# First attention of a two-layer diffusion block: two heads in step, row maxima from the high parts on 64 contraction rows

## The chip, the cores and the metric

The kernel runs on one NeuronCore of a Trainium2 chip. The metric is device time in microseconds (us) of one execution, the median of several runs. All products are made in float32 precision by splitting operands into a high part, which the fp32r format of the matmuls holds exactly, and a low part (the rest), and adding up to three products of parts.

## The reference

Two layers over 1024 latent tokens and 256 context tokens, 1024 features each. Each layer modulates its input, mixes the tokens, projects, adds and normalizes, then runs a gated feed-forward with 2816 hidden features, adds and normalizes again. The mixer of layer 0 holds the attention that the change touches: 12 query heads of 64 features share 4 heads of keys and values (three query heads for each).

```python
def gqa_attend(q, k, v):
    s = jnp.einsum('bkgqd,bksd->bkgqs', q, k, preferred_element_type=F32) * (HEAD_DIM ** -0.5)
    p = jax.nn.softmax(s, axis=-1)
    return jnp.einsum('bkgqs,bksd->bkgqd', p.astype(v.dtype), v)
```

Latent queries attend to all 1280 keys, context queries to the 256 context keys. Queries and keys have been normalized and rotated before. A softmax does not depend on what is subtracted from a row of scores; the row maximum is subtracted to keep the exponentials in range.

## The kernel before

One program runs the stages in order: `in0` (input projections of layer 0; it leaves the heads' queries, keys and values in DRAM, as `qs`, `ks` and `v0`, each with its high part in rows 0 to 63 and its low part in rows 64 to 127), `attn0` (the first attention), `out_proj`, `ffn`, and the same for layer 1 with another attention. A scheduler writes the order of the instructions of each engine: it takes them in the order in which the code emits them, as a priority, and puts an instruction whose inputs or buffers are not ready, by its own estimate of times, behind others that are. On the chip each engine then follows that fixed order.

`attn0` works in units of one head and 256 queries, 60 units: 48 of latents with ten tiles of 128 keys, taken as five steps of two tiles, and 12 of context with one step. Within a pair of heads the units alternate between the two heads. Each step has three parts, emitted at different times:

- `most` computes scores query-major, of the high part of q with both parts of k (128 rows of contraction: `q1` holds the high part of q twice, `kst` both parts of k). Step 0 makes two matmuls of 256 context keys (L926), steps 1 to 4 one matmul of 512 keys each (L931). VectorE reduces each bank to negated row maxima (L927, L932). The last step combines them, splits them in two parts, transposes these on TensorE (L945), and ScalarE writes them as rows 64 and 65 of `q2` (L946).
- `expo` computes the scores again, key-major: for each of two key tiles one matmul on 128 rows (L955) and one on 66 (L956, the low part of q and the two rows that take the maxima off). ScalarE makes the exponentials `e` (L958). They are split into high and low parts in `pp`: the high part is copied by GpSimd or ScalarE, the low part subtracted by GpSimd or VectorE, as the step's letters in `HENG0` and `LENG0` say (helpers at L205, L209 and L213).
- `pv` multiplies the parts with the values, three matmuls for each key tile (L972, L973, L974; `va` has the high part of v and 64 columns of ones, which give the sums of a row, `vb` the low part). After the last step `fin` copies the result to SBUF (L984), transposes the row sums with two matmuls that have one row of contraction, at partition 64 (L987), takes their reciprocals, spreads them over 64 partitions with two transposes (L991), multiplies (L995) and, for every second head, splits the two heads' 128 features into `X` on GpSimd.

`most` is emitted 6 steps ahead of `expo` (`LEAD0`) and `pv` 4 steps behind it (`LAG0`). PSUM has 8 banks: 3 for the scores of `most`, 2 for those of `expo`, 1 for the values, 2 for transposes. `load` fetches the queries of a unit, and keys and values when a new head of them begins, on SP's queue. Other work may be emitted between the steps by `pump`, from a queue that `ada_vec` fills; for this stage `ADA0[1]` is empty, and `in0` ends with emptying the queue.

Of the kernel before, what the change touches and what calls it, by code (L numbers as in the profile page):

```python
# [9 lines left out]
F32 = mybir.dt.float32  # L10
# [7 lines left out]
P = 128  # L18
# [34 lines left out]
HENG0, LENG0, LEAD0, LAG0, PB0 = 'gagaa', 'ggvgv', 6, 4, (3, 2, 2)  # L53
# [20 lines left out]
# ------------------------------------------------------------------ host side: layout only  # L74
# [101 lines left out]
class K:  # L176
# [48 lines left out]
    # ---- weights: one unit of [128, 1024] float32 -> exact (h, l) pair  # L225
# [79 lines left out]
    def ada_vec(self, l, v, nvec, srcs, pspool, pstag, bufs=2, q0=0, abufs=None):  # L305
        """queue modulation vector v of layer l (for nvec of the two conditionings), feature-major"""
# [32 lines left out]
    # ---------------------------------------------------------------- residual, layer norm  # L339
# [6 lines left out]
    def acc_load(self, l, c, b):  # L346
        """ALPHA * x of feature chunk c, block b"""
# [12 lines left out]
    def ln_block(self, b, pools, sc=None, sh=None, acc='keep', out=None, lnb=None, eng=None, tiles=None, group=1):  # L360
        """LN of the columns of block b of ACC (normalised token-major, in place): X = split(LN * sc + sh), ACC = ALPHA * LN."""
# [48 lines left out]
    def ln_vecs(self, l, lng, lnb, nvec, ml, vsh, vsc, tag):  # L410
        """per conditioning: s = g * (1 + sc), b' = b * (1 + sc) + sh ; and ALPHA * g, ALPHA * b"""
# [22 lines left out]
    def qk_post(self, wp, pst, ps, tt, dst, h0, norm, tabs, lat, gain):  # L434
        """ps [128, 512] = 2 token tiles x 4 heads x 64; tt the first token tile; writes dst[h0..h0+3]"""
# [50 lines left out]
    def v_post(self, wp, ps, tt, dst, h0, dv, tag="t1", bufs=2):  # L486
        """ps [128, 2 x 256] to dst [head][128 tok][kt]: (h | l) of 64 columns each, or 128 float32 columns"""
# [17 lines left out]
    def tm_mm(self, o, w, kh, i):  # L505
        """256 output columns of token tile i over one half of the contraction; o: a half of a bank"""
# [39 lines left out]
    def early(self, l, pp, wp):  # L546
        """first hidden chunks of the first blocks, beside the last layer norm of the out-projection"""
# [12 lines left out]
    def ffn(self, l, blks):  # L560
# [3 lines left out]
        with tc.tile_pool(name=f"ffn{l}", bufs=1, reuse_waits="tile") as fp:  # L564
# [11 lines left out]
            def hidden(hc):  # L576
                """hidden chunk hc: {block: (h, l) parts}"""
# [26 lines left out]
            # hidden chunks in pairs; the last ones run block by block beside the layer norm  # L604
# [84 lines left out]
    # ---------------------------------------------------------------- out-projection of both mixers  # L689
# [41 lines left out]
    # ---------------------------------------------------------------- layer 0  # L731
    def in0(self):
# [8 lines left out]
        with ExitStack() as es:  # L741
# [35 lines left out]
            # rope tables with the gains: (q, k) x (cos, sin)  # L777
# [16 lines left out]
            # u: pool mixer branch, feature-major  # L794
# [13 lines left out]
            def pool_mat():  # L808
                """grouped pool matrix, in place"""
# [26 lines left out]
    def pool_mix_sums(self, wp, dp, j, u, pin, ped):  # L836
        nc = self.nc
        L = PADL
        if True:
# [13 lines left out]
            # rows that stopped a step earlier lie in the other buffer  # L853
# [11 lines left out]
    def dup_load(self, dst, src):  # L865
        """dst [128, n] = src [64, n] twice"""
# [3 lines left out]
    def pt_mm(self, psg, es_, i):  # L870
        """transposes of key tiles i, i+1 of two query tiles into one bank"""
# [7 lines left out]
    def attn0(self):  # L879
        """Scores twice: query-major (high part of q) for the row maxima, then key-major with the maxima  # L880
        taken off by two more rows of the contraction, so that the exponentials come out key-major."""
        nc, tc = self.nc, self.tc
        with ExitStack() as es:
# [10 lines left out]

            def load(st):
                hd, pr = st['hd'], st['pr']
                kv = hd // 3
                st['q2'] = self.tile(sp, [66, 256], F32R, "q2", bufs=4)
                if kv not in kv_tiles:
                    kst = self.tile(self.kvp, [P, NTOK], F32R, "kst", bufs=2)  # L900
                    self.dma(kst, self.ks[kv])
                    k2 = self.tile(wp, [66, NTOK], F32R, "k2", bufs=2)
                    self.dma(k2[0:64], self.ks[kv, 0:64])
                    self.copy(ONEE[0], k2[64:66], one[64:66, 0:1].to_broadcast([2, NTOK]))
                    va = self.tile(wp, [P, 10, P], F32R, "va", bufs=2)
                    self.dma(va[:, :, 0:64], self.v0[kv, :, :, 0:64])
                    self.copy(ONEE[1], va[:, :, 64:], one.unsqueeze(1).to_broadcast([P, 10, 64]))
                    vb = self.tile(wp, [P, 10, 64], F32R, "vb", bufs=2)
                    self.dma(vb, self.v0[kv, :, :, 64:])
                    kv_tiles[kv] = (kst, k2, va, vb)  # L910
                st['kv'] = kv_tiles[kv]
                st['q1'] = self.tile(self.kvp, [P, 256], F32R, "q1", bufs=4)
                self.dup_load(st['q1'], self.qs[hd, 0:64, pr * 256:pr * 256 + 256])
                self.dma(st['q2'][0:64], self.qs[hd, 64:128, pr * 256:pr * 256 + 256])

            def most(st, i):
                """query-major scores of one bank, its row maxima"""
                if i == 0:
                    load(st)
                    st['m'] = self.tile(sp, [P, 2, 3], F32, "m", bufs=4)  # L920
                S = self.tile(psm, [P, 512], F32, "sm")
                kst = st['kv'][0]
                lhs = lambda t: st['q1'][:, t * P:t * P + P]
                if i == 0:
                    for t in range(2):
                        nc.tensor.matmul(S[:, t * 256:t * 256 + 256], lhsT=lhs(t), rhs=kst[:, NLAT:], start=True, stop=True)  # L926
                    nc.vector.tensor_reduce(out=st['m'][:, :, 0], in_=S.rearrange("p (t k) -> p t k", t=2), axis=AX.X, op=ALU.max,  # L927
                                            negate=True)
                else:
                    t, k = (i - 1) // 2, (i - 1) % 2  # L930
                    nc.tensor.matmul(S, lhsT=lhs(t), rhs=kst[:, k * 512:k * 512 + 512], start=True, stop=True)  # L931
                    nc.vector.tensor_reduce(out=st['m'][:, t, 1 + k:2 + k], in_=S, axis=AX.X, op=ALU.max, negate=True)  # L932
                if i == st['np'] - 1:
                    with tc.high_priority(HP0) if HP0 else ExitStack():
                        if i:
                            m = self.tile(sp, [P, 2], F32, "mm", bufs=4)
                            nc.vector.tensor_reduce(out=m, in_=st['m'], axis=AX.X, op=ALU.min)
                        else:
                            m = st['m'][:, :, 0]
                        r = self.tile(sp, [P, 2, 2], F32R, "mr", bufs=4)  # L940
                        nc.vector.tensor_copy(out=r[:, :, 0], in_=m)
                        nc.vector.tensor_tensor(out=r[:, :, 1], in0=m, in1=r[:, :, 0].bitcast(F32), op=ALU.subtract)
                        S = self.tile(psr, [P, 512], F32, "r")
                        for t in range(2):
                            nc.tensor.transpose(S.bitcast(F32R)[0:2, t * P:t * P + P], r[:, t, :], self.identr)  # L945
                        nc.scalar.copy(out=st['q2'][64:66], in_=S[0:2, :256])  # L946

            def expo(st, i):
                """key-major scores less the maxima, exponentials, their parts"""
                kst, k2 = st['kv'][:2]  # L950
                S = self.tile(pss, [P, 512], F32, "ss")
                for a in range(2):
                    k = (st['k0'] + 2 * i + a) * P
# [374 lines left out]
```

## Time and profile before

| | |
|---|---|
| time, median of 3 runs | 3291.66 us (3290.71 to 3294.64) |
| span of the profiled execution | 3289.0 us |
| its own time beside the span | not recorded; the median is 2.7 us above the span |
| TensorE busy (matmuls) | 3193.6 us, 97% |
| TensorE weight loads | 2815.5 us, 86%, beside the matmuls |
| VectorE, ScalarE, GpSimd busy | 55%, 31%, 41% |
| granted TensorE clock, mean | 0.984 of full speed |
| first attention | about 288 to 705 us |

The profile lists instructions by line, engine, operation and tile. Busy time is the time covered by an engine's recorded instructions. A matmul's record runs to the modelled end of its results, and the next one starts earlier than that, so the distance between starts says more of TensorE's pace than the recorded length. A matmul of fp32 data appears as two records, a weight load (PEld) and the matmul (PE).

### The profile page before, as it was taken

The numbers are of one execution on the slowest core, as the hardware profiler recorded it, in microseconds if no ns is written. First come the engines' busy times: TensorE is split into PE (matmuls) and PEld (weight loads), VectorE is DVE, ScalarE is ACT, GpSimd is POOL, SyncE is SP. The second block draws the span as 40 slices with busy tenths as digits, with TensorE's granted clock in tenths as the row PEclk, the third lists the DMA queues.
The fourth block names the chain that finished last, engine by engine and source line by source line (L and its number), as shares of the span: only waits on it lengthen the run. The fifth ranks groups of instructions, "written<-read, shape, count | busy, mean of one in ns | idle before, by whom it ended". The sixth has DMA issues, their size and how long they took to land. (4 is left out here: it accounts for less than half of the span.)

```text
span 3289.0 us, 47600 instructions
## 1 busy us (share of the span) xinstructions
PE 3193.6 (97%) x18820; PEld 2815.5 (86%) x18820; DVE 1825.3 (55%) x3251; ACT 1011.1 (31%) x1800; POOL 1352.9 (41%) x1266
## 2 busy tenths in 40 slices
PE   8899999999999999999999989999999999999997
PEld 8798999988888888888888889988887888888887
DVE  6998777766655444443226696378854323222326
ACT  2235676642310111111113333377842211111111
POOL 3665777761322222222222244267742332232234
PEclk8899999999999999999999999999999999999999
DMA  5354021031222222221112144222320111111111
GB/s 224 108 189 121 28 51 54 28 134 56 89 72 77 78 73 70 70 77 52 39 39 65 66 132 139 92 76 84 90 93 24 58 52 45 52 46 51 45 58 52
DMA packets 142895, 250.60 MB, mean 76 GB/s; under 512 B 25552, under 2 KB 95952, under 8 KB 142544
## 3 DMA queue, kind: packets, MB, share of 16 engines
q1 hardware_dynamic: 142672, 247.55, 23.6%
q8 instruction: 149, 2.44, 0.3%
q14 instruction: 74, 0.61, 0.1%
HBM read 207.91 MB, written 39.58 MB: 75 GB/s over the span
## 5 line engine op out<-in xcount | busy, mean ns | idle before, releaser
L213 POOL TENSOR_TENSOR w<-raw,w 128x1024 fp32r<-128x1024 f32 x120 | 288.1, 2408 | 820.5 <-ACT w L205 572.5
L235 PE MATMUL f<-X,w 128*128 128x512 f32 (+1 forms) x1648 | 607.9, 369 | 1.2 <-ACT ACC L217 1.2
L236 PE MATMUL f<-X,w 128*128 128x512 f32 (+1 forms) x1648 | 605.2, 367 | 0.0
L237 PE MATMUL f<-X,w 128*128 128x512 f32 (+1 forms) x1648 | 604.9, 367 | 0.0
L205 ACT CAST w<-raw 128x1024 fp32r<-128x1024 f32 x176 | 182.4, 1049 | 1019.2 <-issue 615.0
L540 DVE TENSOR_TENSOR sg<-f,sg 128x512 f32<-128x512 f32 (+1 forms) x103 | 65.2, 633 | 589.8 <-ACT sg L539 589.8
L358 DVE SCALAR_TENSOR_TENSOR ACC<-f,mod,ACC 128x512 f32<-128x512 f32 (+1 forms) x400 | 274.1, 695 | 164.3 <-PE f L237 164.2
L235 PEld LDWEIGHTS f<-X,w 128*128 128x128 f32 x1648 | 311.5, 189 | 52.1 <-ACT ACC L217 1.6
L237 PEld LDWEIGHTS f<-X,w 128*128 128x128 f32 x1648 | 311.3, 189 | 51.6
L236 PEld LDWEIGHTS f<-X,w 128*128 128x128 f32 x1648 | 311.5, 189 | 50.3
L513 PE MATMUL acc<-w,X 128*128 128x256 f32 x1008 | 292.9, 291 | 8.5 <-ACT u L802 4.9
L324 DVE SCALAR_TENSOR_TENSOR ada<-adraw,silu_c,ada 128x256 f32<-128x256 f32 x490 | 290.7, 630 | 5.9 <-DMA adraw<-in_ad 2.9
L514 PE MATMUL acc<-w,X 128*128 128x256 f32 x1008 | 291.6, 289 | 0.0
L515 PE MATMUL acc<-w,X 128*128 128x256 f32 x1008 | 291.5, 290 | 0.0
L236 PE MATMUL f<-hid,w 128*128 128x512 f32 (+1 forms) x776 | 283.6, 367 | 0.0
L237 PE MATMUL f<-hid,w 128*128 128x512 f32 (+1 forms) x776 | 283.4, 367 | 0.0
L235 PE MATMUL f<-hid,w 128*128 128x512 f32 (+1 forms) x776 | 282.1, 367 | 0.0
L213 POOL TENSOR_TENSOR hid<-sg,hid 128x512 fp32r<-128x512 f32 (+1 forms) x109 | 132.2, 1213 | 303.4 <-DVE hid L207 292.1
L213 POOL TENSOR_TENSOR pp<-e,pp 128x512 fp32r<-128x512 f32 x156 | 203.8, 1314 | 34.8 <-ACT pp L205 29.0
L513 PEld LDWEIGHTS acc<-w,X 128*128 128x128 f32 x1008 | 198.0, 197 | 9.4 <-ACT u L802 5.1
L514 PEld LDWEIGHTS acc<-w,X 128*128 128x128 f32 x1008 | 198.1, 196 | 0.0
L515 PEld LDWEIGHTS acc<-w,X 128*128 128x128 f32 x1008 | 197.8, 196 | 0.0
(279 smaller groups left out, 7026.4 us busy)
## 6 DMA issues: line engine op xcount, KB each, us to landing
raw<-in_fi SPq DMA_DIRECT2D x88, 512.0 KB, 3.6
adraw<-in_ad SPq DMA_DIRECT2D x86, 512.0 KB, 3.7
raw<-in_fo SPq DMA_DIRECT2D x44, 512.0 KB, 3.6
qs<-stg SPq DMA_DIRECT2D x27, 512.0 KB, 3.9
qd<-qs SPq DMA_DIRECT2D x192, 64.0 KB, 2.3
q<-qs SPq DMA_DIRECT2D x180, 64.0 KB, 2.2
ks<-stg SPq DMA_DIRECT2D x20, 512.0 KB, 3.0
kst<-ks SPq DMA_DIRECT2D x16, 640.0 KB, 4.3
```

The lines of the kernel that those rows point to most:

```text
L205: nc.scalar.copy(out=out, in_=in_)
L213: eng.tensor_tensor(out=out, in0=a, in1=b, op=op)
L235: mm(ps, lhsT=wh, rhs=xh, start=start, stop=False)
L236: mm(ps, lhsT=wh, rhs=xl, start=False, stop=False)
L237: mm(ps, lhsT=wl, rhs=xh, start=False, stop=stop)
L324: nc.vector.scalar_tensor_tensor(out=a, in0=rv[:, k], scalar=s, in1=a, op0=ALU.mult, op1=ALU.add)
L358: self.nc.vector.scalar_tensor_tensor(out=a, in0=ps[:, :n], scalar=g[:, f:f + 1], in1=a, op0=ALU.mult, op1=ALU.add)
L513: mm(o, lhsT=xh, rhs=w[:, 0, k], start=st, stop=False)
L514: mm(o, lhsT=xh, rhs=w[:, 1, k], start=False, stop=False)
L515: mm(o, lhsT=xl, rhs=w[:, 0, k], start=False, stop=sp)
L540: nc.vector.tensor_tensor(out=sg[:, :n], in0=pa[:, :n], in1=sg[:, :n], op=ALU.mult)
```

## The change

The units become pairs of heads: 30 units (24 of latents, 6 of context), each with five or one step, and every step does its work for both heads. `most` uses the high part of k alone, on 64 rows of contraction: the even head's matmul has its operands in partitions 0 to 63, the odd head's in partitions 64 to 127, where `q1` has the second copy of q's high part and a new tile `ku` a copy of k's. The matmuls of the two heads are emitted next to each other, into two banks. Their maxima lie in one tile, so that combining, splitting and transposing come once for both heads. `expo` and `pv` loop over the heads; both heads of a step use the same engines for their parts. The values of the two heads share one bank, half each. `fin` comes once for both heads: one copy of 512 columns, four transposes of sums in one bank and four spreading transposes in another. `LAG0` goes from 4 steps to 2 (steps are twice as large), the `e` tiles from 5 to 3, `q1` and `q2` from 4 of one head to 3 of each head, `os` and `on` from 2 to 1. The call of `pump` in the loop is removed. The rest of the diff takes comments and docstrings out.

```diff
-HENG0, LENG0, LEAD0, LAG0, PB0 = 'gagaa', 'ggvgv', 6, 4, (3, 2, 2)
+HENG0, LENG0, LEAD0, LAG0, PB0 = 'gagaa', 'ggvgv', 6, 2, (3, 2, 2)
...
+            def load_kv(kv):
...
+                ku = self.tile(wp, [P, NTOK], F32R, "ku", bufs=2)
+                self.dma(ku[64:128], self.ks[kv, 0:64])
...
             def most(st, i):
...
-                S = self.tile(psm, [P, 512], F32, "sm")
-                kst = st['kv'][0]
-                lhs = lambda t: st['q1'][:, t * P:t * P + P]
+                S = [self.tile(psm, [P, 512], F32, "sm") for j in range(2)]
+                rows = [slice(0, 64), slice(64, 128)]
+                kh = [st['kv'][0][0], st['kv'][1][2]]
+                lhs = lambda j, t: st['q1'][j][rows[j], t * P:t * P + P]
                 if i == 0:
                     for t in range(2):
-                        nc.tensor.matmul(S[:, t * 256:t * 256 + 256], lhsT=lhs(t), rhs=kst[:, NLAT:], start=True, stop=True)
...
+                        for j in range(2):
+                            nc.tensor.matmul(S[j][:, t * 256:t * 256 + 256], lhsT=lhs(j, t), rhs=kh[j][rows[j], NLAT:],
+                                             start=True, stop=True)
...
                     t, k = (i - 1) // 2, (i - 1) % 2
-                    nc.tensor.matmul(S, lhsT=lhs(t), rhs=kst[:, k * 512:k * 512 + 512], start=True, stop=True)
-                    nc.vector.tensor_reduce(out=st['m'][:, t, 1 + k:2 + k], in_=S, axis=AX.X, op=ALU.max, negate=True)
+                    for j in range(2):
+                        nc.tensor.matmul(S[j], lhsT=lhs(j, t), rhs=kh[j][rows[j], k * 512:k * 512 + 512], start=True, stop=True)
+                    for j in range(2):
+                        nc.vector.tensor_reduce(out=st['m'][:, j, t, 1 + k:2 + k], in_=S[j], axis=AX.X, op=ALU.max, negate=True)
...
             def expo(st, i):
...
+                for j in range(2):
...
-                e = self.tile(wp, [P, 512], F32, "e", bufs=5)
+                    e = self.tile(wp, [P, 512], F32, "e", bufs=3)
...
             def pv(st, i):
...
+                po = [st['po'][:, j * 256:j * 256 + 256] for j in range(2)]
...
+                    for j in range(2):
+                        va, vb = st['kv'][j][3:]
+                        h, l = [st['p'][i, j][:, s, a * 256:a * 256 + 256] for s in range(2)]
+                        nc.tensor.matmul(po[j], lhsT=va[:, k], rhs=h, start=i + a + j == 0, stop=False)
+                        nc.tensor.matmul(po[j][0:64], lhsT=vb[:, k], rhs=h, start=False, stop=False)
+                        nc.tensor.matmul(po[j], lhsT=va[:, k], rhs=l, start=False, stop=i == st['np'] - 1 and a + j == 2)
...
             def fin(st):
...
-                os = self.tile(wp, [P, 256], F32, "os", bufs=2)
-                nc.scalar.copy(out=os, in_=po[:, :256])
+                os = self.tile(wp, [P, 512], F32, "os", bufs=1)
+                nc.scalar.copy(out=os, in_=po)
                 R = self.tile(psr, [P, 512], F32, "r")
-                for t in range(2):
-                    nc.tensor.transpose(R[:, 256 + t:257 + t], os[64:65, t * P:t * P + P], self.ident[64:65, 64:65])
...
+                for t in range(4):
+                    nc.tensor.transpose(R[:, t:t + 1], os[64:65, t * P:t * P + P], self.ident[64:65, 64:65])
...
-            units = [dict(hd=2 * hp + j, pr=pr, k0=0 if pr < 4 else NLAT // P, np=5 if pr < 4 else 1, p={})
-                     for hp in range(6) for pr in range(5) for j in range(2)]
+            units = [dict(hp=hp, pr=pr, k0=0 if pr < 4 else NLAT // P, np=5 if pr < 4 else 1, p={})
+                     for hp in range(6) for pr in range(5)]
...
-                if n % ADA0[2] == 7:
-                    self.pump(1)
```

## Rows read from the trace of the kernel before

**Rows 1.** The page, part 1: busy us (share of the span) xinstructions.
```profile
PE 3193.6 (97%) x18820; PEld 2815.5 (86%) x18820; DVE 1825.3 (55%) x3251; ACT 1011.1 (31%) x1800; POOL 1352.9 (41%) x1266
```

**Rows 2.** Busy time by windows: stretch, length, engines, granted clock, DMA share.
```profile
core 0: us, PE busy (x) PEld busy (x) DVE busy (x) ACT busy (x) POOL busy (x), PEclk, DMA share, GB/s
...
300.00:700.00 400.00, 400.00 (x3128) 374.92 (x3127) 296.91 (x605) 272.85 (x512) 303.85 (x320) 1.00 0.14 37
```

**Rows 3.** Waits, 300 to 705 us: who, for whom; total us, times, longest.
```profile
ACT e L958 <- PE ss L956: 78.2, 127, 2.8
...
DVE m L927 <- PE sm L926: 37.1, 34, 1.9
...
PEld o L974 <- DVE pp L213: 0.2, 1, 0.2
```

**Rows 4.** Timeline of TensorE's matmuls: start us, length us, instruction.
```profile
422.46 0.63 PE L931 MATMUL sm<-kst,q 128*128 128x512 f32 x2
422.94 0.28 PE L955 MATMUL ss<-q,kst 128*128 128x256 f32 x1
423.05 0.29 PE L956 MATMUL ss<-q,k 66*128 66x256 f32 x1
423.17 0.29 PE L955 MATMUL ss<-q,kst 128*128 128x256 f32 x1
423.30 0.28 PE L956 MATMUL ss<-q,k 66*128 66x256 f32 x1
423.51 0.28 PE L987 MATMUL r<-c_ident,os 1*128 1x1 f32 x2
423.72 0.39 PE L972 MATMUL o<-pp,va 128*128 128x256 f32 x1
423.94 0.28 PE L973 MATMUL o<-pp,vb 128*64 128x256 f32 x1
424.06 0.28 PE L974 MATMUL o<-pp,va 128*128 128x256 f32 x1
```

**Rows 5.** Groups by line, 285 to 710 us: busy us, mean ns | idle before.
```profile
L213 POOL TENSOR_TENSOR pp<-e,pp 128x512 fp32r<-128x512 f32 x156 | 203.8, 1314 | 34.8 <-ACT pp L205 29.0 <-DVE m L932 1.3
...
L931 PE MATMUL sm<-kst,q 128*128 128x512 f32 x192 | 73.0, 418 | 2.2 <-DVE m L927 1.5 <-DVE m L932 0.5 <-ACT ps_d L816 0.3
L209 POOL TENSOR_SCALAR pp<-e 128x512 fp32r<-128x512 f32 x108 | 72.7, 674 | 69.8 <-ACT e L958 69.3 <-PE ss L956 0.4
...
L926 PE MATMUL sm<-kst,q 128*128 128x256 f32 x120 | 26.4, 301 | 0.0
```

**Rows 6.** Timeline of TensorE's weight loads in the stretch of rows 4.
```profile
423.18 0.19 PEld L956 LDWEIGHTS ss<-q,k 66*128 66x128 f32 x1
423.51 0.19 PEld L987 LDWEIGHTS r<-c_ident,os 1*128 1x128 f32 x2
423.72 0.19 PEld L972 LDWEIGHTS o<-pp,va 128*128 128x128 f32 x1
```

**Rows 7.** One line, L987: matmuls with first and last start; idle before.
```profile
L987 PE MATMUL r<-c_ident,os x120: 194/217/221, 308.7 to 704.4; 1*128 1x1 f32 x120
...
  issue: 8.0, 32
```

**Rows 8.** Timeline of matmuls where L945 stands between L987's.
```profile
308.37 0.40 PE L931 MATMUL sm<-kst,q 128*128 128x512 f32 x1
308.70 0.22 PE L987 MATMUL r<-c_ident,os 1*128 1x1 f32 x1
308.84 0.28 PE L945 MATMUL r<-identr,mr 128*2 128x128 f32 x2
...
309.43 0.28 PE L973 MATMUL o<-pp,vb 128*64 128x256 f32 x1
```

**Rows 9.** Timeline of VectorE at the attention's start.
```profile
288.09 0.62 DVE L927 TENSOR_REDUCE m<-sm 128x2 f32<-128x512 f32 x1
...
292.82 0.14 DVE L937 TENSOR_REDUCE mm<-m 128x2 f32<-128x6 f32 x1
```

**Rows 10.** DMA issues, 280 to 710 us: count, KB each, us to landing.
```profile
k<-ks SPq DMA_DIRECT2D x4, 320.0 KB, 5.3
```

More of the change, by code (lines that the diff above doesn't have):

```diff
@@ L893, in attn0 @@
             kv_tiles = {}
-            def load(st):
[L896 to L914, printed above, removed]
@@ new lines, in load_kv @@
+            def load_kv(kv):
+                kst = self.tile(self.kvp, [P, NTOK], F32R, "kst", bufs=2)
+                self.dma(kst, self.ks[kv])
+                k2 = self.tile(wp, [66, NTOK], F32R, "k2", bufs=2)
+                self.dma(k2[0:64], self.ks[kv, 0:64])
+                self.copy(ONEE[0], k2[64:66], one[64:66, 0:1].to_broadcast([2, NTOK]))
+                ku = self.tile(wp, [P, NTOK], F32R, "ku", bufs=2)
+                self.dma(ku[64:128], self.ks[kv, 0:64])
+                va = self.tile(wp, [P, 10, P], F32R, "va", bufs=2)
+                self.dma(va[:, :, 0:64], self.v0[kv, :, :, 0:64])
+                self.copy(ONEE[1], va[:, :, 64:], one.unsqueeze(1).to_broadcast([P, 10, 64]))
+                vb = self.tile(wp, [P, 10, 64], F32R, "vb", bufs=2)
+                self.dma(vb, self.v0[kv, :, :, 64:])
+                return kst, k2, ku, va, vb
@@ new lines, in load @@
+            def load(st):
+                pr = st['pr']
+                st['kv'], st['q1'], st['q2'] = [], [], []
+                for j in range(2):
+                    hd = 2 * st['hp'] + j
+                    kv = hd // 3
+                    if kv not in kv_tiles:
+                        kv_tiles[kv] = load_kv(kv)
+                    st['kv'].append(kv_tiles[kv])
+                    q2 = self.tile(sp, [66, 256], F32R, f"q2{j}", bufs=3)
+                    q1 = self.tile(self.kvp, [P, 256], F32R, f"q1{j}", bufs=3)
+                    self.dup_load(q1, self.qs[hd, 0:64, pr * 256:pr * 256 + 256])
+                    self.dma(q2[0:64], self.qs[hd, 64:128, pr * 256:pr * 256 + 256])
+                    st['q1'].append(q1)
+                    st['q2'].append(q2)
@@ L935, in most @@
                         if i:
[L936 removed]
+                            m = self.tile(sp, [P, 2, 2], F32, "mm", bufs=4)
                             nc.vector.tensor_reduce(out=m, in_=st['m'], axis=AX.X, op=ALU.min)
                         else:
[L939 to L941 removed]
@@ L946, in most @@
-                        nc.scalar.copy(out=st['q2'][64:66], in_=S[0:2, :256])
-            def expo(st, i):
[L950 to L953, printed above, removed]
-                    o = S[:, a * 256:a * 256 + 256]
-                    nc.tensor.matmul(o, lhsT=kst[:, k:k + P], rhs=st['q1'], start=True, stop=False)
-                    nc.tensor.matmul(o, lhsT=k2[:, k:k + P], rhs=st['q2'], start=False, stop=True)
-                e = self.tile(wp, [P, 512], F32, "e", bufs=5)
-                nc.scalar.activation(e, S, AF.Exp)
-                p = st['p'][i] = self.tile(wp, [P, 2, 512], F32R, "pp", bufs=6)
-                self.copy(HENG0[i], p[:, 0], e)
-                self.tt(LENG0[i], p[:, 1], e, p[:, 0].bitcast(F32), ALU.subtract)
+                        for j in range(2):
+                            for t in range(2):
+                                o = j * 256 + t * P
+                                nc.tensor.transpose(S.bitcast(F32R)[0:2, o:o + P], r[:, j, t, :], self.identr)
@@ new lines, in most @@
+                        for j in range(2):
+                            nc.scalar.copy(out=st['q2'][j][64:66], in_=S[0:2, j * 256:j * 256 + 256])
+            def expo(st, i):
+                for j in range(2):
+                    kst, k2 = st['kv'][j][:2]
+                    S = self.tile(pss, [P, 512], F32, "ss")
+                    for a in range(2):
+                        k = (st['k0'] + 2 * i + a) * P
+                        o = S[:, a * 256:a * 256 + 256]
+                        nc.tensor.matmul(o, lhsT=kst[:, k:k + P], rhs=st['q1'][j], start=True, stop=False)
+                        nc.tensor.matmul(o, lhsT=k2[:, k:k + P], rhs=st['q2'][j], start=False, stop=True)
+                    e = self.tile(wp, [P, 512], F32, "e", bufs=3)
+                    nc.scalar.activation(e, S, AF.Exp)
+                    p = st['p'][i, j] = self.tile(wp, [P, 2, 512], F32R, "pp", bufs=6)
+                    self.copy(HENG0[i], p[:, 0], e)
+                    self.tt(LENG0[i], p[:, 1], e, p[:, 0].bitcast(F32), ALU.subtract)
@@ L965, in pv @@
                     st['po'] = self.tile(pso, [P, 512], F32, "o")
-                va, vb = st['kv'][2:]
-                po = st['po'][:, :256]
+                po = [st['po'][:, j * 256:j * 256 + 256] for j in range(2)]
                 for a in range(2):
                     k = st['k0'] + 2 * i + a
-                    h, l = [st['p'][i][:, s, a * 256:a * 256 + 256] for s in range(2)]
-                    last = i == st['np'] - 1 and a == 1
-                    nc.tensor.matmul(po, lhsT=va[:, k], rhs=h, start=i == 0 and a == 0, stop=False)
-                    nc.tensor.matmul(po[0:64], lhsT=vb[:, k], rhs=h, start=False, stop=False)
-                    nc.tensor.matmul(po, lhsT=va[:, k], rhs=l, start=False, stop=last)
+                    for j in range(2):
+                        va, vb = st['kv'][j][3:]
[3 more added lines that the diff above has]
+                        nc.tensor.matmul(po[j], lhsT=va[:, k], rhs=l, start=False, stop=i == st['np'] - 1 and a + j == 2)
@@ L985, in fin @@
                 R = self.tile(psr, [P, 512], F32, "r")
-                for t in range(2):
-                    nc.tensor.transpose(R[:, 256 + t:257 + t], os[64:65, t * P:t * P + P], self.ident[64:65, 64:65])
-                rz = self.tile(sp, [P, 2], F32, "rz", bufs=2)
-                nc.vector.reciprocal(out=rz, in_=R[:, 256:258])
-                for t in range(2):
-                    nc.tensor.transpose(R[0:64, t * P:t * P + P], rz[:, t:t + 1].to_broadcast([P, 64]), self.ident)
-                if r == 0:
-                    on[pr] = self.tile(wp, [P, 256], F32, "on", bufs=2)
@@ new lines, in fin @@
+                rz = self.tile(sp, [P, 4], F32, "rz", bufs=2)
+                nc.vector.reciprocal(out=rz, in_=R[:, 0:4])
+                R = self.tile(psr, [P, 512], F32, "r")
+                for t in range(4):
+                    nc.tensor.transpose(R[0:64, t * P:t * P + P], rz[:, t:t + 1].to_broadcast([P, 64]), self.ident)
+                o = self.tile(wp, [P, 256], F32, "on", bufs=1)
+                for j in range(2):
+                    nc.vector.tensor_tensor(out=o[j * 64:j * 64 + 64, :], in0=os[0:64, j * 256:j * 256 + 256],
+                                            in1=R[0:64, j * 256:j * 256 + 256], op=ALU.mult)
```

25 lines of the change are left out of this document (11 added, 14 removed).

## The prediction

> **What bounds the kernel now.** I read the busy shares of the page first, then the stretch that the change touches, then who waits for whom in it, then single instructions. Over the whole span TensorE is busy 97% of the time and no other engine above 55% [rows 1]. The first attention runs from its first reduction at 288 us to its last transposes at 704 us [rows 7, 9]. In its steady part, 300 to 700 us, TensorE is busy in all 400 us at the full granted clock; VectorE is busy 297, ScalarE 273 and GpSimd 304 us of them [rows 2]. The waits say the same: ScalarE stands 78.2 us for scores, VectorE 37.1 us for the first bank of the maxima, while the one wait of TensorE for the parts of the exponentials comes to 0.2 us [rows 3]. So this stage is as long as TensorE's list of instructions; a microsecond added to or taken from that list is a microsecond of the kernel, and one on another engine is worth nothing until that engine makes TensorE wait.
>
> Busy time does not price that list, because matmuls overlap: a 256-column matmul is recorded as 0.28 us, but the next one starts 0.12 us later. I therefore use distances between starts. A 256-column matmul takes 0.118 us (422.94 to 423.30 is three of them), a 512-column one 0.235 us (two from 422.46 to 422.94) [rows 4].
>
> **The maxima's matmuls, the heart of the change.** Before, the 192 matmuls of 512 columns (L931) and 120 of 256 (L926) [rows 5] use all 128 rows. They cost 192 x 0.233 = 44.7 and 120 x 0.118 = 14.2 us. After it there are as many, each on 64 rows, the even head's in rows 0 to 63, the odd head's in 64 to 127. They come in blocks: 96 of two 512-column matmuls and 30 of four 256-column ones (24 units of latents and 6 of context). A block is surrounded by matmuls on all rows.
>
> What entering and leaving such a block costs has one near row: the two transposes of L987, which use one row at partition 64. From the last full matmul (423.30) to the second full one behind them (423.94) it is 0.64 us, where two full matmuls take 0.236: the two one-column transposes cost 0.40 us [rows 4]. The weights show why. A full-row weight load starts with the matmul before it (0.12 us ahead of its own matmul); that of L987 starts 0.33 us after the load before it, and that of the matmul behind it again not before 423.72, with the matmul's own start [rows 6]. So the load is no longer hidden, in either direction. Neither the 66 rows of L956 nor the 64 output columns of L973 do this (0.12 us each [rows 4]), so it is the partial rows that do. The engine waits there for nothing that the profile shows, 32 times for 8.0 us [rows 7].
>
> [...]
>
> Now the blocks. Bounds: at best no switch cost and two halves side by side, at worst the full switch and halves one after the other. I take the switch of L987, 0.40 us (which has in it the 0.08 us or so by which the second load follows the first), and halves that run side by side.
> - A pair of 512 columns: 0.40 + 0.235 = 0.635 against 0.466 now, +0.17; 96 pairs: +16.3 us.
> - A first step of four: the weight loads follow each other 0.08 us apart and each half of the rows streams twice, so that it ends some 0.29 us later than the two transposes: 0.40 + 0.29 = 0.69 against 0.47, +0.22; 30 of them: +6.5 us.
> Together +22.8 us. One after the other it would be 96 x (0.40 + 0.47 - 0.47) + 30 x 0.40 = +50 us. Without a switch cost, side by side but with the second load 0.08 us later, 96 x (0.315 - 0.466) + 30 x (0.37 - 0.47) = -17.5 us, and with no such delay half of 44.7 + 14.2, -29.5 us.
>
> [...]
>
> **The ends of the units.** L987's 120 transposes [rows 7] come 60 times by two now, 30 times by four after the change. Adjacent pairs cost 0.40; where the maxima's transposes (L945) stand between them, 308.37 to 309.43 is 1.06 us for work that takes 0.47 without them, so 0.59 [rows 8]. Some 30 us go there now (counted along the timeline: 21 clean at 0.40, 31 split at 0.59, 8 beside other things, put at 0.5). Thirty fours cost 0.40 + 2 x 0.08 = 0.56 clean and 0.75 split, 17 to 23 us. I take -10 us (bounds -4 and -13). The other transposes keep their number. One copy of 512 columns on ScalarE takes the place of two of 256, and the small VectorE operations on the maxima come half as often: nothing, since those engines have 100 us to spare [rows 2].
>
> **Start.** The first exponentials need the maxima of a whole unit. Before they are five reductions, from 288.09 to 292.82, of 0.6 us each [rows 9]; after it ten, +3 us; part of this is lead work that must be done anyway. +2 us (0 to 5). The copy ku adds one 320 KB load for each of 4 heads of keys, and q1 and q2 are as many transfers as before; the DMA engines are 14% busy here [rows 2]: nothing; if that cover were gone, some 5 us for each load, by the 5.3 us of the like one to k [rows 10].
>
> **Rhythm.** Both heads use one engine for the same step, so GpSimd gets 2 x (0.67 + 1.31) = 4.0 us in step 0 and 2 x 1.31 = 2.6 us in step 1 [rows 5], 6.6 us besides the last unit's split into X, while TensorE's two steps last 2 x (20 x 0.118 + 0.6) = 5.9 us. Steps 2 to 4 give that back. The distance from scores to values stays (two steps of 3.0 us for four of 1.5), the e tiles go from 5 to 3 and one bank still takes the values. Behind a late part stand the value matmuls, and behind them the whole of TensorE. Cover gone, 24 units lose about 1 us each; by the 0.2 us of now, nothing. I take +2 us, near that row, and keep 0 to 24. The removed pump has nothing to emit here: no modulation vector is queued for this stage.
>
> **Sum.** +22.8 - 10 + 2 + 2 = +17 us. The profiled span of 3289.0 us is 0.1% below the median of 3291.66; the difference is added to the median: 3308 us.
>
> **The rivals.**
> - *Halves overlap and nothing drains* (faster). For it: L973 and L956 change shape for free [rows 4]. Against: L987, the only partial-row form, never does. -17.5 - 10 + 4 = -24, 3268 us; down to 3256 without the delay of the second load. It decides where a block costs less than 0.47 us.
> - *A wash.* The switch costs only what a lone transpose of L987 does, about 0.29 us (half of 0.59 [rows 8]), and the halves start together: 0.29 + 0.235 = 0.52 a pair, +0.06 x 96 + 0.05 x 30 = +7, less 10, plus 4: 3293 us.
> - *The change doesn't do what it says*: the halves run one after the other (+50 - 10 + 4, 3336 us), or the order written by the scheduler parts them, so that each pays a switch of its own (2 x 0.29 + 0.47 for 0.47, +0.58 x 96 = +56 for the pairs alone, up to 3350 us). The maxima's matmuls stand alone at 308.37 [rows 8] and in twos at 422.46 [rows 4], so either order occurs.
> - *Late parts*: +20 us more than forecast from the rhythm, 3326 us.
>
> **Chances.** Forecast 0.42, late parts 0.05, one after the other or parted 0.15, wash 0.18, no drain 0.20. A measurement of this kernel tells 0.2%, 6.6 us, from no change. Slower: 0.42 + 0.05 + 0.15 = 0.62. Of the wash 0.14 lies within 0.2% and 0.04 below. Faster: 0.20 + 0.04 = 0.24. The forecast's own range is 3297 to 3322; both signs hold weight, so the range reaches from the no-drain case to the sequential one with some late parts, 3258 to 3345.
>
> **What would show it.** Right: a weight load of the maxima's first half 0.2 us or more behind the last full matmul's start, another gap behind the block, 0.6 to 0.7 us from block to block of a pair; the first attention some 433 us long; TensorE's time before L987 about a third less. Wrong: starts of two halves with the next full matmul 0.25 to 0.35 us behind (no drain), 0.85 us (no overlap), or TensorE idle before the value matmuls for GpSimd (rhythm).

## The result and the profile after

The changed kernel takes 3350.55 us (3347.65 to 3355.31), the kernel before 3292.88 us in the same comparison: 1.0177 times as long, with an interval of 1.0162 to 1.0191. The forecast was 3308 us; the direction was right, the size far off. The profiled execution took 3347.65 us, with a span of 3345.8 us, 56.8 us more than before. The first attention ends at 757 us instead of 704.

The busy shares say almost nothing of this. First the page's part 1, then the stretch of [rows 2], of the kernel after:

```profile
PE 3236.0 (97%) x18820; PEld 2809.1 (84%) x18820; DVE 1815.5 (54%) x3137; ACT 1004.9 (30%) x1770; POOL 1353.0 (40%) x1266
```
```profile
300.00:700.00 400.00, 399.39 (x2760) 332.35 (x2759) 260.76 (x452) 238.18 (x430) 267.22 (x280) 0.98 0.14 36
```

TensorE still counts as busy throughout and still is the bound, but it gets through 2760 matmuls in these 400 us where it did 3128. The other engines have become idler, not later. The waits of 300 to 705 us (who, for whom: total us, times, longest), against [rows 3]; the first line is from the kernel before, the rest from the kernel after:

```profile
DVE m L932 <- PE sm L931: 19.4, 21, 1.7
```
```profile
ACT e L979 <- PE ss L977: 117.8, 119, 2.8
...
DVE m L949 <- PE sm L947: 55.7, 71, 2.6
...
PEld ss L976 <- issue: 8.4, 34, 0.4
...
PEld sm L947 <- issue: 7.7, 41, 0.2
```

ScalarE waits longer for TensorE's scores (117.8 us, 78.2 before), VectorE longer for the 512-column maxima (55.7 us, 19.4 before). New are waits of weight loads for "issue", that is, for nothing that the profile shows: the mark that only L987 carried before [rows 7] now stands at the maxima (L947) and at what comes behind them (L976 above all).

What the order of the matmuls became is the main reading. Two pieces of TensorE's timeline (start us, length us), first a half that stands alone:

```profile
476.72 0.28 PE L977 MATMUL ss<-q,k 66*128 66x256 f32 x1
476.93 0.49 PE L947 MATMUL sm<-kst,q 64*128 64x512 f32 x1
477.36 0.38 PE L976 MATMUL ss<-q,kst 128*128 128x256 f32 x1
477.58 0.28 PE L977 MATMUL ss<-q,k 66*128 66x256 f32 x1
```

Then two halves side by side:

```profile
459.69 0.28 PE L977 MATMUL ss<-q,k 66*128 66x256 f32 x1
459.90 0.49 PE L947 MATMUL sm<-kst,q 64*128 64x512 f32 x1
459.90 0.50 PE L947 MATMUL sm<-ku,q 64*128 64x512 f32 x1
460.33 0.39 PE L976 MATMUL ss<-q,kst 128*128 128x256 f32 x1
460.56 0.28 PE L977 MATMUL ss<-q,k 66*128 66x256 f32 x1
```

From the full matmul ahead to the second full one behind are 0.86 us in the first and 0.87 in the second; less the 0.236 that two full matmuls take, the block costs 0.62 and 0.63 us. A lone half costs as much as a pair. All such blocks along the timeline from 316 us on (a block is a run of partial-row matmuls between two full ones; medians, us; the last column is what the same matmuls take on all rows):

| block | times | cost | same matmuls on all 128 rows |
|---|---|---|---|
| one half of 512 columns | 86 | 0.622 | 0.233 |
| two of 256, same half | 34 | 0.622 | 0.237 |
| two halves of 512 | 19 | 0.628 | 0.466 |
| four of 256 and 512, alternating | 11 | 0.860 | 0.703 |

With a few rarer kinds and those of the start, TensorE enters partial rows for the maxima some 184 times, where the forecast had 126 blocks. The weight loads of the pair show the cost as [rows 6] did for L987:

```profile
459.57 0.19 PEld L977 LDWEIGHTS ss<-q,k 66*128 66x128 f32 x1
459.90 0.18 PEld L947 LDWEIGHTS sm<-kst,q 64*128 64x128 f32 x1
459.90 0.18 PEld L947 LDWEIGHTS sm<-ku,q 64*128 64x128 f32 x1
460.33 0.19 PEld L976 LDWEIGHTS ss<-q,kst 128*128 128x128 f32 x1 [0.25 <-issue]
```

The load of the first half comes 0.33 us after the one before it, and the load behind the block only with its own matmul.

The sums became cheaper, as foreseen. The four transposes of L1005 in a row, against [rows 4]:

```profile
422.35 0.28 PE L977 MATMUL ss<-q,k 66*128 66x256 f32 x1
422.56 0.40 PE L1005 MATMUL r<-c_ident,os 1*128 1x1 f32 x4
422.90 0.39 PE L993 MATMUL o<-pp,va 128*128 128x256 f32 x1
423.12 0.28 PE L994 MATMUL o<-pp,vb 128*64 128x256 f32 x1
```

They cost 0.534 us (0.77 less 0.236); beside a block of maxima they add only some 0.33 us: the two together are one visit to partial rows.

By the same counting from 312 us on, the maxima and sums together took 83.9 us of TensorE's list before and 125.7 after: maxima about 53 and 110, sums about 31 and 15.5. What happens ahead of 312 us, the start, shows in a lag: the time since 285 us, less what the stage's matmuls begun by then take on all rows and at full clock. At 312 us it is 9.9 us before and 18.1 after. The stage ends 53 us later. Of these, 41.8 are the list and 8.2 the start. Cut at 316 us instead, about when the granted clock is back (below), the list gives 42.0 and the start 10.4, so most of the 3 us left over belongs to the start too. Some 4 us behind the stage stay unassigned.

### The profile page after: what moved, and what is told of

Same layout as the page of the kernel before. It is cut to its first block, busy times and chain, and to the rows that moved or that the text cites. A ratio compares the mean times of both kernels' runs of the same rounds, so it can differ in the third digit from the quotient of the medians.

```text
span 3345.8 us, 47440 instructions
## 1 busy us (share of the span) xinstructions
PE 3236.0 (97%) x18820; PEld 2809.1 (84%) x18820; DVE 1815.5 (54%) x3137; ACT 1004.9 (30%) x1770; POOL 1353.0 (40%) x1266
```

## The experiments

The theory: entering and leaving partial rows costs about 0.39 us a block whatever is in it; the order parts the two halves because their banks come free one after the other; halves that do meet run together. Rivals: halves run one after the other; the loss is in the two-heads rhythm, not in the row halves. In the experiments "the list" is the time between starts that maxima and sums take from 312 us on; a wait of TensorE inside it counts with it.

**Two heads in step, all 128 rows.** The changed kernel with `kst` in place of the halves; `ku` is not loaded.

```diff
-                rows = [slice(0, 64), slice(64, 128)]
-                kh = [st['kv'][0][0], st['kv'][1][2]]
+                rows = [slice(0, 128), slice(0, 128)]
+                kh = [st['kv'][0][0], st['kv'][1][0]]
```

> Two heads in step as in the changed kernel, but the maxima's matmuls on all 128 rows as before (ku is not loaded); the one-row transposes of the sums stay, 30 times by four. Theory (parted halves): in the changed kernel a lone 512-column matmul on 64 rows takes 0.62 us of TensorE's list where 0.23 would do, and the start waits 7 us for ku; without both, the stage is the one of before less some 14 us of the sums' switches, plus 4 us for a start on ten reductions: 3282 us (3272 to 3295). Rival (rhythm): two heads in step make the parts late and TensorE waits; then nothing much changes, 3320 us or more. Rival (the start alone): 10 us come back, about 3340.

Measured: 3287.33 us against 3291.83, ratio 0.9988 [0.9979, 0.9998]. Without the row halves the change is a small gain, so its whole loss comes with the 64 rows. The list of maxima and sums is 74.9 us, 9.0 shorter than before, by the sums that come in fours. The rhythm is not quite free here: TensorE idles 5.5 us where it idled none in [rows 2].

```profile
300.00:700.00 400.00, 394.50 (x3165) 374.73 (x3164) 303.30 (x502) 270.24 (x492) 312.36 (x324) 1.00 0.14 36
```

**Halves kept together.** One tile of two banks for both halves, so that they come free at once. `PB0` goes with it: the maxima have two such tiles, four banks where they had three, and the transposes one bank where they had two.

```diff
-HENG0, LENG0, LEAD0, LAG0, PB0 = 'gagaa', 'ggvgv', 6, 2, (3, 2, 2)
+HENG0, LENG0, LEAD0, LAG0, PB0 = 'gagaa', 'ggvgv', 6, 2, (2, 2, 1)
...
-                S = [self.tile(psm, [P, 512], F32, "sm") for j in range(2)]
+                SS = self.tile(psm, [P, 1024], F32, "sm")
+                S = [SS[:, j * 512:j * 512 + 512] for j in range(2)]
```

> The changed kernel with the two banks of a step as one tile (two such tiles, so 4 banks for the maxima and 1 for the transposes in place of 3 and 2): both halves become ready together, and the order written puts them next to each other nearly everywhere (123 blocks in place of 184). Theory (parted halves): a pair costs 0.63 us against 0.47 on all rows, 96 x 0.16 = +16, first steps +5 to +11, sums -14, start +10: 3312 us (3303 to 3322). Rival (rhythm): no gain, 3345 or more; one bank for the transposes could add up to 10 us by either theory. Rival (halves do not really overlap when adjacent): +38 us, 3340 or more.

Measured: 3313.23 us, ratio 1.0066 [1.0049, 1.0083]. About 37 of the 58 us are gone: blocks of maxima fell from 184 to 123, and the list from 125.7 to 90.9 us, while a pair costs what it did. That the halves' neighbourhood is worth this is shown; whether the shared tile or the fourth bank brought them together is not, as no run has four single banks. A pair in TensorE's timeline of this kernel:

```profile
435.54 0.28 PE L978 MATMUL ss<-q,k 66*128 66x256 f32 x1
435.75 0.49 PE L948 MATMUL sm<-kst,q 64*128 64x512 f32 x1
435.75 0.50 PE L948 MATMUL sm<-ku,q 64*128 64x512 f32 x1
436.18 0.39 PE L977 MATMUL ss<-q,kst 128*128 128x256 f32 x1
436.41 0.28 PE L978 MATMUL ss<-q,k 66*128 66x256 f32 x1
```

62 such pairs cost 0.625 us each, five fours of 256 columns 0.626. Even side by side, a pair costs 0.16 us more than the 0.466 on all rows, and this kernel is 25.9 us slower than the one with all rows.

**One head alone on 64 rows.** The kernel before, with only the operands of its maxima cut to rows 0 to 63 (the maxima then come from the high parts; there is no `ku`).

```diff
-                lhs = lambda t: st['q1'][:, t * P:t * P + P]
+                lhs = lambda t: st['q1'][0:64, t * P:t * P + P]
...
-                    nc.tensor.matmul(S, lhsT=lhs(t), rhs=kst[:, k * 512:k * 512 + 512], start=True, stop=True)
+                    nc.tensor.matmul(S, lhsT=lhs(t), rhs=kst[0:64, k * 512:k * 512 + 512], start=True, stop=True)
```

(and the same for the 256 context keys)

> The kernel before, one head at a time, where only the maxima's matmuls change: the high parts of q and k on rows 0 to 63. Theory (partial rows switch the engine): some 169 blocks in the order written, each 0.39 us more than on all rows, and 0.1 us more for each further matmul of a block on the same rows, whose weights are not hidden; less some 8 us where a block stands beside L987: +66 + 15 - 8 = +73, 3365 us (3345 to 3380). Rival (only the pairing costs): 64 rows cost as much as 128, 3290 to 3300 us.

Measured: 3354.36 us, ratio 1.0191 [1.0175, 1.0206]. Nothing here can run side by side, so this prices the switch by itself: 63 lone matmuls of 512 columns cost 0.619 us each for work of 0.233. Two in the same rows:

```profile
444.40 0.28 PE L956 MATMUL ss<-q,k 66*128 66x256 f32 x1
444.61 0.73 PE L931 MATMUL sm<-kst,q 64*128 64x512 f32 x2
445.27 0.39 PE L955 MATMUL ss<-q,kst 128*128 128x256 f32 x1
445.49 0.28 PE L956 MATMUL ss<-q,k 66*128 66x256 f32 x1
```

Their block costs 0.855 us against the pair's 0.625. So halves in different rows do overlap, and the rival "one after the other" falls. The 0.1 us expected for a further matmul on the same rows doesn't show: 0.855 is 0.389 above the 0.466 of two on all rows, and a lone one is 0.386 above its own.

**Blocks of four.** The kernel that keeps the halves together, now with one tile of four banks (`PB0` (1, 2, 1)): steps 1 and 2, and 3 and 4, make their maxima in one block.

```diff
-                SS = self.tile(psm, [P, 1024], F32, "sm")
-                S = [SS[:, j * 512:j * 512 + 512] for j in range(2)]
+                if i in (0, 1, 3):
+                    SS = self.tile(psm, [P, 2048], F32, "sm")
+                    S = [SS[:, b * 512:b * 512 + 512] for b in range(4)]
...
+                elif i in (1, 3):
+                    t = (i - 1) // 2
+                    for k in range(2):
+                        for j in range(2):
+                            nc.tensor.matmul(S[2 * k + j], lhsT=lhs(j, t), rhs=kh[j][rows[j], k * 512:k * 512 + 512], start=True, stop=True)
```

> Maxima on 64 rows, two heads in step, but one tile of four banks (one such tile, 1 bank for the transposes): steps 1 and 2, and 3 and 4, make one block of four 512-column matmuls, alternating between the halves (88 blocks in the order written). Theory (a switch is paid per block, and halves overlap): 0.85 us a block against 0.93 on all rows, 48 x -0.08 = -4 us; first steps +5, start +7 over the pairs on all rows (3287 us): 3295 us (3288 to 3302), so 18 us better than pairs next to each other. Rival (the single tile makes TensorE wait for VectorE's four reductions): 3310 us or more.

Measured: 3305.6 us, ratio 1.0041 [1.0028, 1.0053]; slower than expected. The block itself came out as reckoned:

```profile
455.53 0.28 PE L998 MATMUL o<-pp,vb 128*64 128x256 f32 x1
455.74 0.50 PE L950 MATMUL sm<-kst,q 64*128 64x512 f32 x1
455.74 0.50 PE L950 MATMUL sm<-ku,q 64*128 64x512 f32 x1
456.07 0.39 PE L950 MATMUL sm<-kst,q 64*128 64x512 f32 x1
456.08 0.40 PE L950 MATMUL sm<-ku,q 64*128 64x512 f32 x1
456.40 0.38 PE L999 MATMUL o<-pp,va 128*128 128x256 f32 x1
456.62 0.28 PE L997 MATMUL o<-pp,va 128*128 128x256 f32 x1
```

35 of these fours cost 0.856 us, less than the 0.932 of four on all rows: here row halves pay, by 0.08 us a block. Against the kernel with all rows the list was nevertheless 5.6 us longer (80.5 to 74.9): ten first steps were parted into three matmuls and one, at 0.633 and 0.508 us instead of 0.628 for the four. The start cost 8.6 us more than there. Part of that is the rival named above, that the single tile makes TensorE wait for VectorE's reductions: its matmuls at 299.61 and 303.42 us each come after 2.58 us of such waiting.

```profile
299.61 0.79 PE L950 MATMUL sm<-kst,q 64*128 64x512 f32 x1 [2.58 <-DVE m L953]
```

**The start: the late copy?** The first maxima of the changed kernel waited for `ku`:

```profile
291.40 0.55 PE L939 MATMUL sm<-ku,q 64*128 64x256 f32 x1 [7.00 <-DMA ku<-ks]
```

In the kernel that keeps the halves together, `ku` is loaded right behind `kst`, and `q1` before `k2`, `q2` and the values, which go behind them.

```diff
                 self.dma(kst, self.ks[kv])
+                ku = self.tile(wp, [P, NTOK], F32R, "ku", bufs=2)
+                self.dma(ku[64:128], self.ks[kv, 0:64])
...
+            def load_rest(kv):
+                k2, va, vb = kv_tiles[kv][1], *kv_tiles[kv][3:]
+                self.dma(k2[0:64], self.ks[kv, 0:64])
...
```

> The kernel with adjacent pairs (two-bank tiles), where ku is loaded right behind kst and q1 before k2, q2 and the values, instead of behind k2. Theory (the start waits for ku): TensorE's first wait of 5 to 7 us shrinks by about half, and its clock rises sooner: 3313 - 4 = 3309 us (3304 to 3311). Rival (the 8 us that the start lost come from ten reductions and switches at the low clock, not from ku): no change, 3311 to 3315 us.

Measured: 3313.14 us, ratio 1.0067 [1.0054, 1.0080], the same as without. The lag at 312 us stays (18.3 us, 18.2 before the edit). But the edit hardly took the wait away: the first matmul on `ku` still waits 4.66 us for it, where it waited 5.32. Nor does the clock rise sooner: it is 0.52 from 310 to 315 us, 0.59 before the edit.

```profile
294.02 0.58 PE L947 MATMUL sm<-ku,q 64*128 64x256 f32 x1 [4.66 <-DMA ku<-ks]
```

So this run doesn't show what the wait costs. The lags at 300 us say more: 11.0 us after the change, 10.3 with all rows and no `ku`. By then the wait and the halves together have cost 0.7 us.

**The start: the clock?** Windows of the start (stretch, length, busy us of PE, PEld, DVE, ACT, POOL, granted clock, DMA share, GB/s). The kernel before, after, with all rows, with halves together, and with one head alone on 64 rows:

```profile
305.00:310.00 5.00, 5.00 (x38) 4.40 (x37) 3.22 (x7) 3.55 (x8) 3.91 (x5) 1.00 0.12 39
```
```profile
305.00:310.00 5.00, 5.00 (x17) 3.61 (x15) 4.85 (x7) 2.43 (x4) 3.85 (x5) 0.50 0.00 0
310.00:315.00 5.00, 5.00 (x20) 3.87 (x20) 2.13 (x4) 1.22 (x3) 1.81 (x2) 0.50 0.01 3
```
```profile
305.00:310.00 5.00, 5.00 (x40) 4.49 (x39) 4.45 (x7) 3.49 (x7) 4.80 (x6) 1.00 0.01 3
```
```profile
305.00:310.00 5.00, 5.00 (x21) 3.84 (x20) 4.48 (x10) 3.63 (x6) 2.90 (x4) 0.50 0.00 0
```
```profile
300.00:305.00 5.00, 5.00 (x18) 3.25 (x18) 2.81 (x5) 1.71 (x4) 1.89 (x2) 0.50 0.02 3
305.00:310.00 5.00, 5.00 (x26) 4.63 (x25) 0.91 (x2) 1.81 (x3) 1.89 (x2) 0.63 0.14 39
```

With row halves in step the granted clock is 0.50 here (until 315 us in the kernel after; with halves together 0.59 from 310 to 315 us), and TensorE does 17 and 21 matmuls from 305 to 310 us; with all rows the clock is 1.00, with 38 and 40 matmuls. It isn't idle meanwhile: in the kernel after it counts as busy in all 20 us from 295 to 315 us. Nor is `ku` needed for it: one head alone on 64 rows, which loads none, is at 0.50 until 305 us, where the kernel before has 1.00 from 300 us on [rows 2]. If the 64 rows cause this, the first two units on all rows must mend it:

```diff
-                rows = [slice(0, 64), slice(64, 128)]
-                kh = [st['kv'][0][0], st['kv'][1][2]]
+                full = st['hp'] == 0 and st['pr'] < 2
+                rows = [slice(0, 128)] * 2 if full else [slice(0, 64), slice(64, 128)]
+                kh = [st['kv'][0][0], st['kv'][1][0 if full else 2]]
```

> The kernel with adjacent pairs (two-bank tiles), where the first two units take their maxima on all 128 rows, and all others on 64. Theory (the start loses 8 us because its few 64-row matmuls leave TensorE's clock at half speed until 312 to 315 us, where the kernel before and the pairs on all rows have the full clock back by 300): the clock is back by about 300 us and 7 us return: 3313 - 7 = 3306 us (3303 to 3309). Rival (the loss is the ten reductions that the first exponentials wait for): clock and time as before, 3311 to 3315 us.

Measured: 3305.99 us, ratio 1.0053 [1.0039, 1.0067], 7.2 us below the kernel that it was made from; the intervals of the two ratios, from different chips, overlap. The trace is clearer: the lag at 312 us fell from 18.2 to 12.0 us, and the clock is 0.78 from 300 to 305 us and 1.00 from 305 us on, where it was 0.50 until 310 us. (These units need no `ku` either, so the run alone would not part the two; the one head on 64 rows does.)

```profile
305.00:310.00 5.00, 5.00 (x39) 4.42 (x37) 2.48 (x5) 3.18 (x7) 4.42 (x5) 1.00 0.01 3
```

**The sums, first try.** The kernel before, its row sums turned by a matmul on all rows with one column of the identity, to leave out the switch.

```diff
-                    nc.tensor.transpose(R[:, 256 + t:257 + t], os[64:65, t * P:t * P + P], self.ident[64:65, 64:65])
+                    nc.tensor.matmul(R[:, 256 + t:257 + t], lhsT=os[:, t * P:t * P + P], rhs=self.ident[:, 64:65], start=True, stop=True)
```

> The kernel before, where the row sums are brought to the queries by a matmul on all 128 rows with one column of the identity, in place of the transposes on one row (L987). Theory (partial rows switch the engine): the 31.7 us that the 120 transposes take of TensorE's list become some 120 x 0.11 = 13 us: 3274 us (3268 to 3282). Rival (the gap at L987 is a wait for the copy os, or comes of its single column): no change, 3290 to 3294 us.

Measured: 3292.62 us, ratio 1.0002 [0.9993, 1.0011]: no change, a miss. The line's instructions:

```profile
L987 PE MATMUL r<-c_ident,os x240: 164/250/271, 309.2 to 704.2; 128*128 128x1 f32 x120
```

Each of the 120 float32 matmuls became two instructions, each with its own weight load; two sums next to each other cost 0.448 us, not less than the 0.406 of two one-row transposes. The question remained open.

**The sums, second try.** A transpose of the whole tile, of which column 64 is used.

```diff
-                    nc.tensor.transpose(R[:, 256 + t:257 + t], os[64:65, t * P:t * P + P], self.ident[64:65, 64:65])
+                    nc.tensor.transpose(R[:, 256 + t * P:256 + t * P + P], os[:, t * P:t * P + P], self.ident)
...
-                nc.vector.reciprocal(out=rz, in_=R[:, 256:258])
+                nc.vector.reciprocal(out=rz, in_=R[:, 256:].rearrange("p (t k) -> p t k", t=2)[:, :, 64])
```

> The kernel before, where the row sums come by a transpose of all 128 rows of os (128 columns moved, of which one is used) in place of L987's on one row. The run with a 1-column matmul on all rows did not gain, as each such matmul of plain float32 is two instructions of 0.11 us; a transpose is one, as L991 shows (0.109 us). Theory (partial rows switch the engine): 120 x 0.109 = 13 us in place of 31.7, -18 us: 3274 us (3270 to 3282). Rival (the time at L987 is not the rows but waiting for os): 3290 to 3294 us.

Measured: 3281.13 us, ratio 0.9968 [0.9957, 0.9979], faster than both kernels. It is one instruction each (120 for 120), and of the 8.0 us of waiting for "issue" at L987 [rows 7] none is left. Two of them in the timeline:

```profile
426.66 0.40 PE L931 MATMUL sm<-kst,q 128*128 128x512 f32 x1
426.90 0.38 PE L987 MATMUL r<-c_ident,os 128*128 128x128 f32 x2
427.03 0.36 PE L972 MATMUL o<-pp,va 128*128 128x256 f32 x1
427.23 0.28 PE L973 MATMUL o<-pp,vb 128*64 128x256 f32 x1
```

Two cost 0.228 us instead of 0.406, though each writes 128 columns instead of one. The list got some 12 us shorter, the kernel 10; in 300 to 700 us TensorE now stands idle for 4 us, one of them behind the stage's end at 695 us:

```profile
300.00:700.00 400.00, 395.93 (x3169) 378.06 (x3167) 320.01 (x612) 274.19 (x517) 311.34 (x325) 1.00 0.14 40
```

**Both heads in step on all rows, sums by full transposes.** The same edit in the kernel of the first experiment, four transposes to a bank.

> Two heads in step, maxima on all 128 rows, sums by full transposes, so no partial rows anywhere. Theory (partial rows switch the engine): 30 blocks of four one-row transposes (17 to 20 us) become 13 us: 3287 - 6 = 3281 us (3276 to 3286). Rival (with no switches left, late parts bound the stage): no gain over the 3287 us of the pairs with one-row sums.

Measured: 3287.99 us, ratio 0.9990 [0.9981, 0.9999]: a miss, no better than without the edit. The trace has TensorE busy for less:

```profile
300.00:700.00 400.00, 392.14 (x3157) 377.08 (x3155) 296.54 (x500) 266.29 (x488) 311.34 (x325) 1.00 0.14 36
```

Its longest waits there are the value matmuls' loads for VectorE's parts of the exponentials (3.2 us in 3 waits). That fits the rival of late parts, but no run takes that wait away, so it stays argued. The traces also place the miss elsewhere: the stage ends at 698 us, 2 us earlier than in the first experiment, and what follows it takes 3.5 us longer, for a reason that no run shows. Against one head at a time with the same transposes the stage ends 2.6 us later; that is what two heads in step cost where no partial rows are left.

**The best of the row halves.** Blocks of four, first two units on all rows, full transposes, together.

> All that the runs show put together for maxima on 64 rows: blocks of four in one four-bank tile, the first two units on all rows, sums by full transposes. Theory (each block costs 0.39 us and what its busier half streams): 3306 for blocks of four, -8 for the start, -5 for the sums: 3293 us (3288 to 3299), so still no gain over the maxima on all rows (3281 for one head at a time, 3288 for pairs). Rival (row halves pay once blocks are large and the start is mended): 3280 us or less.

Measured: 3296.9 us, ratio 1.0021 [1.0011, 1.0030], as expected. Even so the halves don't pay.

## Why the prediction was right or wrong

- *TensorE's list is the time, and it grows.* Right: TensorE idles 0.6 us of 400 after the change, and the list and the start account for 50 of the stage's 53 us.
- *The price of a switch, 0.40 us, taken from L987.* Right: 0.39 us a block. A lone half takes 0.622 us where a 512-column matmul on all rows takes 0.233, and a pair 0.628 where one such matmul takes 0.235. No pair of the kernel after came under the 0.47 us that the rival "nothing drains" needed; the least was 0.536. What the engine does in the 0.39 us is not shown.
- *A pair costs 0.635 us, side by side.* Right where a pair exists: 0.628 after, 0.625 with a shared tile. The two halves start 0.004 us apart (459.900 and 459.904 us). That they run side by side was an assumption of the author's, which nothing in the kernel before shows. Against two matmuls on the same half, 0.855 us, running together saves 0.23 us a pair; entering and leaving costs 0.39.
- *A first step of four, 0.69 us.* Too dear: 0.626.
- *"They come in blocks: 96 of two 512-column matmuls and 30 of four 256-column ones."* This step failed. The diff emits the halves next to each other, and I took emission for the order on the engine, although [rows 4, 8] show the matmuls of the maxima now in twos, now alone. 184 blocks in place of 126, about half of them lone halves at the price of a pair, made the term of the maxima +57 us (from 312 us on) instead of +22.8. Keeping them together gave back 37 us. Why the scheduler puts other work between the halves is likely the three single banks, of which the second half's comes free later; that reason is argued and not shown. The case was among the rivals, with about the right result (up to 3350 us), partly by luck: it parted all 96 pairs and priced a lone half at 0.52 us, where about half were parted and a lone half took 0.62.
- *The sums, -10 us (-4 to -13).* Too little: about -16. The bounds left out that a four beside a block of maxima shares its visit to partial rows, and adds 0.33 us instead of 0.53.
- *The start, +2 us (0 to 5).* Wrong: +8.2 by 312 us, 10.4 by 316. The forecast counted reductions and left out the clock, which stays at 0.50 until 315 us; in the kernel with halves together, all rows in the first two units took 6.2 us of the lag back.
- *Rhythm, +2 us.* Nothing of it shows in the changed kernel, where TensorE idles 0.6 us. It does where the list is shorter: 5.5 us idle with all rows, and a stage 2.6 us longer than one head at a time when no partial rows are left.
- *The copy `ku`, nothing.* About right, though the first matmul did wait 7.0 us for it: by 300 us the lag is 0.7 us above that of the kernel without `ku`. No run took the wait away with the halves kept.

## What to carry to other kernels

Matmuls on 64 rows, among matmuls on all rows, cost this kernel 0.39 us a visit, while those on 66 rows (L956) follow at the usual 0.12 us. At 0.235 (0.625 less 0.39) against 0.466 us for a pair of 512 columns, a visit pays, by an estimate from these numbers, only with more than 0.39 / 0.231 = 1.7 pairs in it; one pair lost 0.16 us and two gained 0.08. So count visits in the final order, not matmuls. Where two instructions must run side by side, look in the trace for whether they still do: here 86 halves of 512 columns stood alone, and 19 blocks were pairs. One-row transposes cost more here than moving the whole tile, 0.406 against 0.228 us for two: doing the whole tile was the best version, at 3281.13 us.

## What was not expected of the hardware

- Within a block a second round of halves starts 0.33 us after the first (455.74 to 456.07), although matmuls of 512 columns on all rows follow each other in 0.235 [rows 4]. The block as a whole still grows by only 0.23 us (0.625 to 0.856).
- The float32 matmul with one column came out as two instructions (240 for 120), the transpose of the same tile as one (120 for 120).
- The granted clock stayed at 0.50 until 315 us in the kernel after, though TensorE counted as busy in all 20 us before that, and was 1.00 from 305 us on in the run with the first units on all rows. What ties the clock to the rows is not shown.
